# Modulation blocks moved beside the merge gates, fins held back by a count of banks, and a fixed joining time behind generators' products, in a two-layer diffusion backbone on one core

## The chip, the cores and the metric

The kernel runs on one core of a Trainium2 chip. The metric is the device time in microseconds (us). TensorE (PE in the profile) does the matrix products, VectorE (DVE) and ScalarE (ACT) the elementwise work and the reading of PSUM, GpSimd (POOL) a little of both, and SyncE's queue (SP) issues the loads.

## The reference, cut to what matters

512 tokens (256 of context, 256 latent) of width 2048 pass two layers. A layer's norm is modulated by shift and scale, and its output by a gate; all three come from a product of a 2048-vector (one for context, one for latent) with `ada_w`:

```python
shift_l, scale_l, gate_l = jnp.split((jax.nn.silu(c) @ ada_w[l] + ada_b[l])[:, None, :], 3, axis=-1)
xn_l = rmsnorm(h_lat, norm_g[l]) * (1.0 + scale_l) + shift_l
out_l, _, v_l = stream_mixer(xn_l, xn_l @ w_in[l], p, vf_lat, grid_shift, s_ctx, True)
h_lat = h_lat + gate_l * out_l
```

`stream_mixer` runs a recurrence over the tokens in both directions for 16 heads (branch A), a pooling mixer (branch B), multiplies each branch by an output matrix (`w_out_a`, `w_out_b`), weighs them with sigmoid merge gates (32 column blocks of `w_in`), adds them, and multiplies with `w_out`. In the second layer the context part ends in the state, so its outputs have 256 columns and not 512.

## The kernel before

The program is written out by a planner in Python, which keeps a clock for each engine (`E["pe"]` and so on), counts the cost of every instruction that it writes, and decides from that which comes next. What it writes is the order on each engine; on the chip the engines wait by semaphores alone.

**Main.** The large products are units in a queue (`M.q2`, and `M.q1` for those that the recurrence calls for). A unit `proj` is one block of 128 output rows; it has chunks of four 128x128 weight blocks, and each step is three matmuls (fp32 split in a high and a low fp32r part: high by high, high by low, low by high). The raw weights come by SP through a ring of three slots `wr` (512 KB each). Units write to two PSUM banks (`pmm`) in turn.

**Generators.** The recurrence is written as generators: `chain` (the walk over 8 blocks of 64 tokens for each of 8 head pairs; three product groups a block), `inv` (an inverse by doubling; some 16 product groups for each half of a pair), `prep`, `gnorm`, `open_y`. A generator yields the time at which its next step is due. Before a product that is the operand's planned time and a margin on top, `MG`, 1000 ns in layer 0 and 600 ns in layer 1. `run` (line 535 on) takes a generator whose time has come; if there is none it writes two steps of Main (six matmuls) and looks again.

**Modulation blocks.** `ada_w` is cut into 24 blocks of 256 columns for each layer: blocks 0 to 15 hold shift and scale, blocks 16 to 23 the gate. `ada_block` multiplies one as raw fp32, 4 chunks of 512 KB, each chunk four small matmuls that run beside each other in four column groups of the array. At its end (`post`) four copies bring the four partial rows to one tile `ada_r` (two on ACT, two on DVE), and a `fin` later sums them with two matmuls by `comb` and writes `modv`. With n = 2 a pair of blocks shares one bank, one set of copies and one fin. The blocks stand so:

- layer 0, blocks 0 to 15: pairs, beside the first projections (`grp`)
- layer 0, blocks 16 to 21: singly, each zipped with one merge gate product (`fillers`, only gates with i = 1); blocks 22 and 23: a pair by itself ahead of the `w_b` products (`tail`)
- layer 1, blocks 0 to 15: pairs, zipped with the 16 `w_o` products of layer 0 (`phase_b`), in banks of `piv`
- layer 1, blocks 16 and 17: a pair between the layers; 18 to 21 singly in `fillers`; 22 and 23 a pair in `tail`

`zipped` interleaves the chunks of two units, takes both units' banks before the first chunk and runs both posts after the last. `Main.step` forces all but one fin out before a unit's `pre`.

**Tail.** `open_y` starts when Main stands at a unit marked as tail; it loads the eight halves of `y_b` through four slots, splits them (`parts`), and sets `open` when all eight are written; the `w_b` units wait for `open`.

Of the kernel before, what the change touches and what calls it, by code (L numbers as in the profile page):

```python
# [18 lines left out]
T = 512  # L19
# [8 lines left out]
SC = 1024.0  # L28
WR, WH, LA, SA = 3, 3, 6, 3
NS, SL = 2, 1000  # L30
NU = (0, 1)
ZD = (0, 0)
N1, LA0, G0, LAG = 2, 20, 2, 4
AH, PACE, MG = 400.0, 600.0, (1000.0, 600.0)

V_MU, V_W0, V_A0, V_KK, V_KA, V_RK = 0, 24, 40, 56, 64, 80
# [10 lines left out]
def kernel(  # L47
# [105 lines left out]
    xn_p, py = Slots(xn_p), Slots(py)  # L153
    wr_p, wh_p, wl_p = Slots(wr_p, WR), Slots(wh_p, WH), Slots(wl_p, WH)
    pmm, piv, pch = Slots(pmm, 2), Slots(piv, 3), Slots(pch, 2)

    def psum(ap):
        return nm(ap).startswith("ps_")
# [7 lines left out]
    def mm(out, lhsT, rhs, start=True, stop=True, dep=True):  # L166
        nc.tensor.matmul(out=out, lhsT=lhsT, rhs=rhs, start=start, stop=stop)  # L167
        n, m = size(rhs), size(lhsT)
        dt = lhsT.dtype
        if dt == F32:  # L170
            c = 110 if m <= 32 else 360 if n < 32 else 1.6 * n if n > 64 else 190 if m > 64 else 78
        elif dt == R32:
            c = max(0.4225 * n, 109) + 75 * (kind[0] != dt)
        else:
            c = 28 if m > 64 else 18
        kind[0] = dt
        clk("pe", c, out, (lhsT, rhs) if dep else (), 200.0)

    kind = [R32]

    def act(out, in_, func=AF.Copy, scale=1.0, bias=None):
        kw = {} if bias is None else dict(bias=bias)
# [44 lines left out]
            late.remove(fins[0])  # L227
            fins[0][1]()

    def later(t, fn):  # L230

        x = (t, fn)
        late.append(x)
        return x

# [109 lines left out]
                    c.update(grp=dict(src=c["src"]), sl=None)  # L345
            self.ready, self.hold, self.tail = ready, hold, False

    def zipped(a, b):

        na, nb = len(a.chunks), len(b.chunks)  # L350
        order = sorted([((i + 0.5) / na, 0, i) for i in range(na)] + [((i + 0.5) / nb, 1, i) for i in range(nb)])
        pos = {(w, i): j for j, (_, w, i) in enumerate(order)}
        steps = [(pos[w, i], f) for w, u in ((0, a), (1, b)) for i, f in u.steps]

        def pre():
            for u in (a, b):
                if u.pre:
                    u.pre()

        def post():  # L360
            for u in (a, b):
                if u.post:
                    u.post()
        return Unit([(a, b)[w].chunks[i] for _, w, i in order], steps, pre, post, a.need, False, a.ready, a.hold)

    class Main:

# [81 lines left out]
        def time(self):  # L449

            self.ahead()
            if self.mi >= len(self.seq):
                return None
            c = self.seq[self.mi]
            u = c["u"]
            if c["first"] and c["pos"] == 0 and u.ready and not u.ready():
                return None
            if c["last"] and c["pos"] == len(c["steps"]) and u.need and not u.need():
                return None
            return rdy(c["r"]) if c["raw"] else rdy(c["h"], c["l"])  # L460

        def step(self):
            c = self.seq[self.mi]
            u = c["u"]
            if c["first"] and c["pos"] == 0 and u.pre:
                flush_fins(1)
                u.pre()
            if c["pos"] < len(c["steps"]):
                c["steps"][c["pos"]][1](c)
                c["pos"] += 1  # L470
            if c["pos"] == len(c["steps"]):
                if c["last"] and u.need and not u.need():
# [17 lines left out]
    def proj(src, nk, rhs, ts_, post, ck=4, **kw):  # L490
        st = {}
        n = ts_.stop - ts_.start

        def pre():
            st["ps"] = pmm.tile([128, T], F32, tag="mm", name="ps_mm")
# [19 lines left out]

    def run():

        while True:
            do_late()
            best, bt, held = None, None, True  # L520
            for g in gens:
                while g[1] is None:
                    g[1] = next(g[0], "end")
                    if g[1] is None:
                        break
                    held = False
                if g[1] == "end" or g[1] is None:
                    continue
                t = due(g[1])
                if best is None or t < bt:  # L530
                    best, bt = g, t
                if t <= E["pe"]:
                    best, bt = g, t
                    break
            gens[:] = [g for g in gens if g[1] != "end"]
            if best is None or bt > E["pe"]:
                mt = M.time()
                if mt is not None and (best is None or max(mt, E["pe"]) <= bt):
                    for _ in range(NS):
                        M.step()  # L540
                        do_late()
                        mt = M.time()
                        if mt is None or mt > E["pe"] + SL:
                            break
                    continue
            if best is None:
                if not gens and M.empty():
# [3 lines left out]
                elif held:  # L551
                    raise RuntimeError("stuck")
                continue
            E["pe"] = max(E["pe"], bt)
            best[1] = next(best[0], "end")
        do_late(True)


    def ada_blocks(l, b0, n, after=None, pre0=None, bank=None, slot=None):


        st = {}
        return [ada_block(l, b0, i, n, st, after, pre0 if i == 0 else None, bank, slot) for i in range(n)]

    def ada_block(l, b0, i, n, st, after, pre0, bank, slot):
        b = b0 + i
        nr = 2 * n

        def pre():
            if pre0:  # L570
                pre0()
            if i == 0:
                pl, tg = bank or (pmm, "mm")
                st["ps"] = pl.tile([128, T], F32, tag=tg, name="ps_ada")

        def mk(j):
            def step(c):
# [5 lines left out]
        def post():  # L583
# [3 lines left out]
            for g in range(4):  # L587
# [2 lines left out]
                    cp(ada_r[q], st["ps"][q, 0:256])  # L590
                else:
                    act(ada_r[q], st["ps"][q, 0:256])
            fins.append(later(rdy(ada_r), fin))

        def fin():

# [26 lines left out]


    def norm_sum(acc, ncol, ones):
        nc.gpsimd.memset(ones, 1.0)
        ps = piv.tile([128, T], F32, tag="iv", name="ps_nrm")
        mm(ps[:, 0:ncol], ones, acc)
        return ps[:, 0:ncol]
# [19 lines left out]
    def phase_a(l):  # L649
# [118 lines left out]
        def mix_unit(g, h):  # L768
# [1 line left out]
            st = {}  # L770

            def pre():
                st["ps"] = pmm.tile([128, T], F32, tag="mm", name="ps_mix")

            def step(c):
                for q in range(2):
# [498 lines left out]
        def open_y():  # L1275
# [7 lines left out]
            for i in range(len(todo) + 3):  # L1283
# [10 lines left out]
                if i == NP + 2:  # L1294
                    keep["open"] = True

        def load_g(f):
            if f < KD:
# [74 lines left out]
        def fillers(ada):  # L1373
# [15 lines left out]
        def tail(ada):  # L1389
# [111 lines left out]
    with tc.manual_schedule():  # L1501
# [185 lines left out]
```

## Time and profile before

| | us |
|---|---|
| three runs | 3054.97, 3052.19, 3052.75 (median 3052.75) |
| profiled execution | 3058.09 |
| its span, first to last instruction | 3056.3 |
| TensorE busy in the span | 2906.3 (95%) |
| VectorE busy | 1820.7 (60%) |
| ScalarE busy | 1457.3 (48%) |
| mean granted TensorE clock | 0.978 |

Times in rows are from the span's start. A matmul's busy time overlaps that of the next, so the step from one start to the next start is what it costs. A wait is put down to what came last. The stages by that clock: start with layer 0's modulation and first projections to about 153, recurrence and its fillers to 1380, a gap to 1401, `w_b` and `w_a` to 1599, `w_o` to 1824, the passage to layer 1 to 1860, its recurrence and fillers to 2829, a gap to 2850, and its last products to the end.

### The profile page before, as it was taken

What the parts mean: (1) busy time and instruction counts of PE and PEld (TensorE: products, weight loads), DVE (VectorE), ACT (ScalarE), POOL (GpSimd) and SP (SyncE); (2) the same over time, 40 slices, a digit from 0 to 9 for tenths busy, and PEclk for the clock granted to TensorE, in tenths of its full rate; (3) what the DMA queues carried; (4) which work ended last, traced back from release to release, by engine and by line L of the source; (5) the groups of instructions that cost most, each with busy time, mean ns of one, the idle gap of its engine ahead of it and who ended that gap; (6) DMA issues with size and microseconds to landing.
All of it is one profiled execution on the core that took longest, in us unless ns stands there. A gap on an engine that the chain in (4) does not pass through costs nothing.

```text
span 3056.3 us, 66262 instructions
## 1 busy us (share of the span) xinstructions
PE 2906.3 (95%) x27122; PEld 2292.5 (75%) x27122; DVE 1820.7 (60%) x4171; ACT 1457.3 (48%) x3092; POOL 149.7 (5%) x211
## 2 busy tenths in 40 slices
PE   5999999999999999998999989999999989999897
PEld 2687777767777777776876657887887768888797
DVE  3475666565655655534443235886786667775575
ACT  3254445445554554533222223666556646666454
POOL 2200000000000000000000002000000000000000
PEclk8999999999999999998999999999999989999899
DMA  9732222232333222327657764432333343344875
GB/s 361 256 121 72 78 76 91 72 116 94 112 111 118 87 80 87 94 88 248 205 190 225 234 222 124 141 117 85 108 94 111 119 127 99 111 122 129 260 251 161
DMA packets 158482, 427.74 MB, mean 140 GB/s; under 512 B 17376, under 2 KB 53600, under 8 KB 154080
## 3 DMA queue, kind: packets, MB, share of 16 engines
q1 hardware_dynamic: 133120, 390.32, 40.5%
q10 hardware_dynamic: 25056, 33.17, 3.0%
q8 instruction: 213, 3.49, 0.5%
q14 instruction: 93, 0.76, 0.1%
HBM read 389.21 MB, written 34.21 MB: 139 GB/s over the span
## 4 chain that ended last, share of the span: by engine, by line
PE 78%; DVE 8%; DMA 7%; ACT 5%; issue 2%; SPq 0%; POOL 0%; DVEq 0%; ACTq 0%; POOLq 0%
PE ps_mm L167 54%; PE ps_st L167 4%; DMA wr<-in_w_o 3%; DVE wlo L191 3%; PE ps_W L167 3%; PE ps_M L167 2%; PE ps_ada L167 2%; PE ps_y L167 2%; PE ps_a L167 2%; DMA wr<-in_w_in 2%; PE ps_Z L167 1%; PE ps_z L167 1%; PE ps_p L167 1%; ACT whi L183 1%; PE ps_T L1113 1%
## 5 line engine op out<-in xcount | busy, mean ns | idle before, releaser
L167 PE MATMUL ps_mm<-xh,whi 128*128 128x512 f32 (+1 forms) x2448 | 914.8, 374 | 8.2 <-ACT whi L183 3.1
L191 DVE TENSOR_TENSOR wlo<-wr,whi 128x512 fp32r<-128x512 f32 (+1 forms) x932 | 636.7, 696 | 444.8 <-ACT whi L183 439.1
L183 ACT ACTIVATE whi<-wr 128x512 fp32r<-128x512 f32 (+1 forms) x932 | 567.1, 619 | 671.3 <-PE ps_mm L167 336.7
L167 PE MATMUL ps_mm<-xh,wlo 128*128 128x512 f32 (+1 forms) x2448 | 855.2, 349 | 16.4 <-DVE wlo L191 15.7
L167 PE MATMUL ps_mm<-xl,whi 128*128 128x512 f32 (+1 forms) x2448 | 851.1, 348 | 0.0
L167 PEld LDWEIGHTS ps_mm<-xh,whi 128*128 128x128 f32 x2448 | 465.6, 190 | 91.9 <-issue 7.9
L167 PEld LDWEIGHTS ps_mm<-xh,wlo 128*128 128x128 f32 x2448 | 465.8, 190 | 83.5 <-DVE wlo L191 22.5
L167 PEld LDWEIGHTS ps_mm<-xl,whi 128*128 128x128 f32 x2448 | 467.6, 191 | 46.3 <-issue 1.0
L167 PE MATMUL ps_mm<-mgh,whi 128*128 128x512 f32 (+1 forms) x512 | 181.2, 354 | 2.9 <-ACT whi L183 2.9
L1024 DVE CAST_PREDICATED X<-pm_t,ps_W 128x128 f16<-128x128 uint8 x640 | 141.7, 288 | 65.2 <-PE ps_W L167 63.8
L167 PE MATMUL ps_mm<-mgh,wlo 128*128 128x512 f32 (+1 forms) x512 | 175.4, 343 | 0.0
L167 PE MATMUL ps_mm<-mgl,whi 128*128 128x512 f32 (+1 forms) x512 | 174.5, 341 | 0.0
L167 PE MATMUL ps_mm<-yh,whi 128*128 128x512 f32 (+1 forms) x512 | 129.0, 344 | 0.2 <-ACT whi L183 0.2
L167 PEld LDWEIGHTS ps_mm<-mgh,whi 128*128 128x128 f32 x512 | 98.2, 192 | 38.9 <-issue 19.3
L167 PE MATMUL ps_mm<-yl,whi 128*128 128x512 f32 (+1 forms) x512 | 125.4, 337 | 0.6 <-DVE m L195 0.5
L183 ACT ACTIVATE VS<-P 64x128 f32<-64x128 f32 x128 | 39.3, 307 | 167.3 <-DVE P L195 164.8
L183 ACT ACTIVATE zb<-ps_Z 128x512 f16<-128x512 f32 x144 | 85.2, 592 | 70.2 <-PE ps_Z L167 68.8
L167 PEld LDWEIGHTS <-X 64*64 64x64 f16 x2560 | 89.4, 110 | 35.7 <-issue 27.5
L191 POOL TENSOR_TENSOR nlo<-MM,n 64x512 f16<-64x512 f32 x48 | 62.8, 1308 | 1072.2 <-DVE X L1024 760.2
L167 PEld LDWEIGHTS ps_mm<-mgh,wlo 128*128 128x128 f32 x512 | 98.3, 192 | 14.5 <-DVE wlo L191 3.6
L167 PEld LDWEIGHTS ps_mm<-mgl,whi 128*128 128x128 f32 x512 | 98.4, 192 | 8.7
L167 PE MATMUL ps_ada<-wr,svp 128*4 128x256 f32 (+1 forms) x1024 | 83.2, 402 | 22.8 <-DMA wr<-in_ada_w 22.8
(258 smaller groups left out, 4353.2 us busy)
## 6 DMA issues: line engine op xcount, KB each, us to landing
wr<-in_w_in SPq DMA_DIRECT2D x306, 512.0 KB, 3.7
wr<-in_ada_w SPq DMA_DIRECT2D x128, 512.0 KB, 3.9
wbig<-in_ada_w SPq DMA_DIRECT2D x32, 1024.0 KB, 6.0
wr<-in_w_o SPq DMA_DIRECT2D x64, 512.0 KB, 4.8
wr<-in_w_b SPq DMA_DIRECT2D x32, 512.0 KB, 4.8
wr<-in_w_a SPq DMA_DIRECT2D x32, 512.0 KB, 4.0
wr<-in_w_st SPq DMA_DIRECT2D x32, 384.0 KB, 4.3
d_mg<-mth ACTq DMA_DIRECT2D x32, 256.0 KB, 2.0
```

The costliest lines, as they stand in the source:

```text
L167: nc.tensor.matmul(out=out, lhsT=lhsT, rhs=rhs, start=start, stop=stop)
L183: nc.scalar.activation(out=out, in_=in_, func=func, scale=scale, **kw)
L191: ENG[eng].tensor_tensor(out=out, in0=a, in1=b, op=op)
L1024: nc.vector.copy_predicated(dst.rearrange(pat, **kw)[:, :, :, u, :], m, src.rearrange(pat, **kw)[:, :, :, u, :])
L1113: nc.tensor.transpose(ps[:, j2, d, :], BK[:, d, c % 4].rearrange("p a t -> p (a t)"), ident)
```

## The change

- In `run`, while products of a generator (or a fin) stand behind the last batch of Main, a generator that is due within `JOIN` = 600 ns of the planner's TensorE clock is taken at once and not after the next two steps of Main. The planner's TensorE clock no longer jumps to the due time for a step with products.
- All gate blocks of layer 0 and blocks 0 to 15 of layer 1 (24) go singly, zipped with merge gates of layer 0: both gates of f = 0 to 7 and the gate i = 1 of f = 8 to 15. Layer 1's blocks 18 to 23 (6) go singly in its fillers. The `tail` pairs and the blocks beside `w_o` are gone. These zips have `lead` 0.25: the modulation chunk stands ahead of the gate's chunk.
- `zipped` calls each unit's `pre` at its own first step and its `post` at its own last step.
- `bank` counts the banks of `pmm` taken, and forces out a fin only when its bank is the one to be taken next. A fin without `after` is due `FD` = 400 ns later than before.
- A `w_b` chunk waits for its own four halves of `y_b` and no more for all eight.
- The memset of `ones` in `norm_sum` (three times in all) moves from GpSimd to VectorE.

```diff
+FD = 400.0
+JOIN = 600.0
+    def bank(name):
+        while fins and fins[0][2] <= taken[0] - 2:
+            flush_fins(len(fins) - 1)
+        taken[0] += 1
+        return pmm.tile([128, T], F32, tag="mm", name=name)
...
-    def zipped(a, b):
+    def zipped(a, b, lead=0.5):
-        order = sorted([((i + 0.5) / na, 0, i) for i in range(na)] + [((i + 0.5) / nb, 1, i) for i in range(nb)])
+        order = sorted([((i + 0.5) / na, 0, i) for i in range(na)] + [((i + lead) / nb, 1, i) for i in range(nb)])
+            def first(c, f=ls[0][1], u=u):
                 if u.pre:
                     u.pre()
+                f(c)
+            def final(c, f=ls[-1][1], u=u):
+                f(c)
                 if u.post:
                     u.post()
...
+            if "ready" in c and not c["ready"]():
+                return None
             if c["first"] and c["pos"] == 0 and u.pre:
-                flush_fins(1)
                 u.pre()
...
+        was = -1
         while True:
             do_late()
+            now = E["pe"] + (JOIN if count[0] != was else 0)
...
-                if t <= E["pe"]:
+                if t <= now:
                     best, bt = g, t
                     break
-            if best is None or bt > E["pe"]:
+            if best is None or bt > now:
...
+                    was = count[0]
                     continue
...
-            E["pe"] = max(E["pe"], bt)
+            n = count[0]
+            if bt > now:
+                E["pe"] = bt
             best[1] = next(best[0], "end")
+            if count[0] == n:
+                E["pe"] = max(E["pe"], bt)
...
-            fins.append(later(rdy(ada_r), fin))
+            fins.append(later(rdy(ada_r) + (0 if after else FD), fin, st["n"]))
...
-        nc.gpsimd.memset(ones, 1.0)
+        nc.vector.memset(ones, 1.0)
...
-                    q.append(zipped(u, ada.pop(0)) if i and ada else u)
+                    q.append(zipped(u, ada.pop(0), 0.25) if (i or len(ada) > KD - 1 - f) and ada else u)
...
-            for u in ada:
-                u.hold, u.tail = free, True
-            q = list(ada)
+            q = []
-                u = proj(w_b[l, f], NP, lambda k: keep["yh"][k], slice(0, nt), post_b(f), hold=free,
-                         ready=lambda: "open" in keep)
+                u = proj(w_b[l, f], NP, lambda k: keep["yh"][k], slice(0, nt), post_b(f), hold=free)
+                for i, c in enumerate(u.chunks):
+                    c["ready"] = lambda i=i: "yh" in keep and all(keep["yh"][4 * i:4 * i + 4])
...
-        M.q2 += A[0]["fillers"](sum((ada_blocks(0, KD + j, 1) for j in range(6)), []))
-        M.q2 += A[0]["tail"](ada_blocks(0, 22, 2))
-        ada1 = sum((ada_blocks(1, b, 2, bank=(piv, "iv")) for b in range(0, KD, 2)), [])
-        qb, B0 = phase_b(0, lambda: A[0], lambda f: hT[f], lambda f: ada1[f])
+        M.q2 += A[0]["fillers"](sum((ada_blocks(0, KD + j, 1) for j in range(8)), []) +
+                                sum((ada_blocks(1, j, 1) for j in range(KD)), []))
+        M.q2 += A[0]["tail"]()
+        qb, B0 = phase_b(0, lambda: A[0], lambda f: hT[f], lambda f: None)
...
-            M.q2 += a["fillers"](sum((ada_blocks(1, KD + N1 + j, 1) for j in range(4)), []))
-            M.q2 += a["tail"](ada_blocks(1, 22, 2))
+            M.q2 += a["fillers"](sum((ada_blocks(1, KD + N1 + j, 1) for j in range(6)), []))
+            M.q2 += a["tail"]()
```

## Rows read from the trace of the kernel before

**Rows 1.** Stretches: us, busy PE, PEld, DVE, ACT, POOL; PEclk, DMA share, GB/s

```profile
153.00:1380.00 1227.00, 1218.37 (x11316) 921.83 (x11315) 720.66 (x1676) 595.70 (x1264) 43.99 (x55) 1.00 0.30 95
1380.00:1401.00 21.00, 7.63 (x72) 2.14 (x70) 8.65 (x14) 7.78 (x14) 0.00 (x0) 0.68 0.80 263
...
1599.00:1824.00 225.00, 214.43 (x1188) 138.71 (x1188) 67.44 (x137) 47.11 (x86) 0.00 (x0) 0.98 0.70 227
...
1860.00:2829.00 969.00, 931.55 (x11091) 796.73 (x11089) 704.87 (x1761) 586.08 (x1317) 62.00 (x78) 0.98 0.38 114
2829.00:2850.00 21.00, 8.67 (x76) 2.96 (x75) 6.79 (x16) 7.36 (x19) 0.00 (x0) 0.64 0.75 242
...
1401.00:1404.60 3.60, 3.60 (x10) 2.92 (x10) 3.40 (x8) 2.09 (x4) 0.00 (x0) 0.50 0.07 16
...
2850.00:2855.20 5.20, 5.20 (x25) 5.20 (x26) 3.75 (x11) 2.16 (x6) 0.00 (x0) 0.50 0.46 129
```

**Rows 2.** TensorE's waits (us, times, longest) in 153:1380, 1599:1824 and, two rows, 1860:2829

```profile
PE ps_ada L167 <- DVE ada_r L206: 4.5, 6, 2.1
...
PE ps_ada L167 <- DVE ada_r L206: 8.7, 7, 1.5
...
PE ps_mm L167 <- DVE wlo L191: 14.4, 15, 2.2
...
PE ps_ada L167 <- DVE ada_r L206: 2.8, 2, 1.8
```

**Rows 3.** Timeline of TensorE: first matmuls of six-matmul stretches, and one group

```profile
256.21 0.50 PE L167 MATMUL ps_mm<-xh,whi 128*128 128x512 f32 x1
...
1299.19 0.50 PE L167 MATMUL ps_mm<-xh,whi 128*128 128x512 f32 x1
...
1979.06 0.28 PE L167 MATMUL ps_mm<-xh,whi 128*128 128x256 f32 x1
...
2789.22 0.28 PE L167 MATMUL ps_mm<-xh,wlo 128*128 128x256 f32 x1
2789.43 0.45 PE L167 MATMUL ps_z<-VS,MM 128*64 128x64 f32 x8
2789.82 0.39 PE L167 MATMUL ps_mm<-xh,whi 128*128 128x256 f32 x1
2790.04 0.28 PE L167 MATMUL ps_mm<-xl,whi 128*128 128x256 f32 x1
2790.16 0.28 PE L167 MATMUL ps_mm<-xh,wlo 128*128 128x256 f32 x1
```

**Rows 4.** Timeline of TensorE around one modulation chunk beside `w_o`

```profile
1819.58 0.39 PE L167 MATMUL ps_mm<-mgh,wlo 128*128 128x512 f32 x1
1819.90 0.61 PE L167 MATMUL ps_ada<-wr,svp 128*4 128x256 f32 x8
1820.44 0.50 PE L167 MATMUL ps_mm<-mgh,whi 128*128 128x512 f32 x1
```

**Rows 5.** Timeline: first and last of one post's four copies, and its fin

```profile
1825.13 0.37 ACT L183 ACTIVATE ada_r<-ps_ada 4x256 f32<-4x256 f32 x1
...
1826.71 0.43 DVE L206 COPY ada_r<-ps_ada 4x256 f32<-4x256 f32 x1 [0.44 <-ACT ada_r L183]
...
1827.54 0.61 PE L167 MATMUL ps_ada<-comb,ada_r 128*128 128x4 f32 x4
```

**Rows 6.** Loads of `y_b` on SP's queue; the page's group of low parts

```profile
1374.36 1.85 SPq L263 DMA_DIRECT2D ldp<-d_yb  x4
...
L191 DVE TENSOR_TENSOR wlo<-wr,whi 128x512 fp32r<-128x512 f32 (+1 forms) x932 | 636.7, 696 | 444.8 <-ACT whi L183 439.1
```

**Rows 7.** The start: TensorE's first products, and two stretches

```profile
22.40 2.07 PE L167 MATMUL ps_nrm<-acc,ones 128*128 128x512 f32 x2 [22.40 <-POOL ones L626]
...
22.00:26.00 4.00, 3.60 (x22) 1.10 (x26) 0.69 (x1) 0.73 (x2) 0.34 (x2) 1.00 1.01 428
26.00:30.00 4.00, 2.80 (x52) 0.91 (x40) 2.58 (x4) 1.62 (x3) 0.00 (x0) 1.00 0.98 346
```

More of the change, by code (lines that the diff above doesn't have):

```diff
@@ L155 @@
     pmm, piv, pch = Slots(pmm, 2), Slots(piv, 3), Slots(pch, 2)
+    taken = [0]
+    def bank(name):
[3 more added lines that the diff above has]
+        return pmm.tile([128, T], F32, tag="mm", name=name)
     def psum(ap):
@@ L176, in mm @@
         kind[0] = dt
+        count[0] += 1
         clk("pe", c, out, (lhsT, rhs) if dep else (), 200.0)
-    kind = [R32]
+    kind, count = [R32], [0]
     def act(out, in_, func=AF.Copy, scale=1.0, bias=None):
@@ L228, in flush_fins, with later @@
             fins[0][1]()
-    def later(t, fn):
-        x = (t, fn)
+    def later(t, fn, n=0):
+        x = (t, fn, n)
         late.append(x)
@@ L346, in __init__ @@
             self.ready, self.hold, self.tail = ready, hold, False
-    def zipped(a, b):
+    def zipped(a, b, lead=0.5):
         na, nb = len(a.chunks), len(b.chunks)
-        order = sorted([((i + 0.5) / na, 0, i) for i in range(na)] + [((i + 0.5) / nb, 1, i) for i in range(nb)])
+        order = sorted([((i + 0.5) / na, 0, i) for i in range(na)] + [((i + lead) / nb, 1, i) for i in range(nb)])
         pos = {(w, i): j for j, (_, w, i) in enumerate(order)}
-        steps = [(pos[w, i], f) for w, u in ((0, a), (1, b)) for i, f in u.steps]
-        def pre():
-            for u in (a, b):
+        steps = []
+        for w, u in ((0, a), (1, b)):
+            ls = [(pos[w, i], f) for i, f in u.steps]
+            def first(c, f=ls[0][1], u=u):
                 if u.pre:
                     u.pre()
-        def post():
-            for u in (a, b):
+                f(c)
+            def final(c, f=ls[-1][1], u=u):
+                f(c)
                 if u.post:
                     u.post()
-        return Unit([(a, b)[w].chunks[i] for _, w, i in order], steps, pre, post, a.need, False, a.ready, a.hold)
+            ls[0] = (ls[0][0], first)
+            ls[-1] = (ls[-1][0], final)
+            steps += ls
+        return Unit([(a, b)[w].chunks[i] for _, w, i in order], steps, None, None, a.need, False, a.ready, a.hold)
     class Main:
@@ L494, in pre @@
         def pre():
-            st["ps"] = pmm.tile([128, T], F32, tag="mm", name="ps_mm")
+            st["ps"] = bank("ps_mm")
         def mk(k):
@@ L553, in run, with ada_blocks, ada_block @@
                 continue
-            E["pe"] = max(E["pe"], bt)
+            n = count[0]
+            if bt > now:
+                E["pe"] = bt
             best[1] = next(best[0], "end")
+            if count[0] == n:
+                E["pe"] = max(E["pe"], bt)
         do_late(True)
-    def ada_blocks(l, b0, n, after=None, pre0=None, bank=None, slot=None):
+    def ada_blocks(l, b0, n, after=None, pre0=None, slot=None):
         st = {}
-        return [ada_block(l, b0, i, n, st, after, pre0 if i == 0 else None, bank, slot) for i in range(n)]
-    def ada_block(l, b0, i, n, st, after, pre0, bank, slot):
+        return [ada_block(l, b0, i, n, st, after, pre0 if i == 0 else None, slot) for i in range(n)]
+    def ada_block(l, b0, i, n, st, after, pre0, slot):
         b = b0 + i
@@ L572, in pre @@
             if i == 0:
-                pl, tg = bank or (pmm, "mm")
-                st["ps"] = pl.tile([128, T], F32, tag=tg, name="ps_ada")
+                st["ps"], st["n"] = bank("ps_ada"), taken[0] - 1
         def mk(j):
@@ L772, in pre @@
             def pre():
-                st["ps"] = pmm.tile([128, T], F32, tag="mm", name="ps_mix")
+                st["ps"] = bank("ps_mix")
             def step(c):
@@ L1293, in open_y @@
                     parts(todo[i - 3][0], todo[i - 3][2], ys[i - 3])
-                if i == NP + 2:
-                    keep["open"] = True
         def load_g(f):
@@ L1385, in fillers, with tail @@
                     u = proj(win(50 + 16 * i + f), KD, rhs, yts, post_mg(i, f))
-                    q.append(zipped(u, ada.pop(0)) if i and ada else u)
+                    q.append(zipped(u, ada.pop(0), 0.25) if (i or len(ada) > KD - 1 - f) and ada else u)
             return q
-        def tail(ada):
+        def tail():
             free = lambda: not M.q1
-            for u in ada:
-                u.hold, u.tail = free, True
-            q = list(ada)
+            q = []
             for f in range(KD):
-                u = proj(w_b[l, f], NP, lambda k: keep["yh"][k], slice(0, nt), post_b(f), hold=free,
-                         ready=lambda: "open" in keep)
+                u = proj(w_b[l, f], NP, lambda k: keep["yh"][k], slice(0, nt), post_b(f), hold=free)
                 u.tail = True
+                for i, c in enumerate(u.chunks):
+                    c["ready"] = lambda i=i: "yh" in keep and all(keep["yh"][4 * i:4 * i + 4])
                 if f == 0:
```

## The prediction, made before the changed kernel was run

> **What bounds the kernel now.** I read the stretches first, to find where TensorE is not the limit, then its waits in each stretch, then the timeline where the change works. In layer 0's recurrence (153 to 1380) TensorE is busy 1218 of 1227 us at full clock, with VectorE at 59% and ScalarE at 49% [rows 1]. So the order of products there costs nothing in waits; what it can still cost is the change from one kind of product to another. In layer 1's recurrence (1860 to 2829) TensorE is busy 932 of 969 us, and VectorE 73%: some 37 us are idle, of which the largest group is low parts of weights (`wlo`) that come late, 14.4 us in 15 waits [rows 1, 2]. Two gaps of 21 us, behind the two recurrences, have TensorE busy 7.6 and 8.7 us, at a mean granted clock of 0.68 and 0.64, with the DMA engines at 0.80 and 0.75 [rows 1]: there the pair of modulation blocks in `tail` runs as fast as its 4 MB come. Beside `w_o` (1599 to 1824) it is fins that TensorE waits for, 8.7 us in 7 waits [rows 2].
>
> **Joined products.** The price of a change of kind is in one group. From the last Main matmul (2789.22) to the group takes 0.21 us where 256 columns step by 0.12 (2790.04 to 2790.16): 0.09 more. The first Main matmul behind it takes 0.22 to the next: 0.10 more [rows 3]. A group that is drawn into the one ahead of it saves 0.19 us. What can be drawn in is what now waits for one batch of Main and then comes at once. Counted in the timeline, 100 stretches of Main between two groups are six matmuls long in layer 0 (the first begins at 256.21, the last at 1299.19) and 145 in layer 1 (1979.06 to 2789.82) [rows 3]. All other stretches are longer: the next step there was due more than a batch later. A 512-column step is 0.23 (0.32 from 1819.58 to 1819.90, less the 0.09 of entering [rows 3, 4]), so a six is 6 x 0.23 + 0.1, about 1.5 us in layer 0. In layer 1, 72 of the 145 are of 256 columns, 0.9 us, and 73 of 512. If the due times lie evenly in these stretches, 600 ns takes 0.4 of 100, 0.67 of 72 and 0.41 of 73: 40 + 48 + 30 = 118 groups, 118 x 0.19 = 22.4 us. Bounds: none of them, 0; all 245, 46.6 us.
>
> Against it stands what a joined product waits for. In layer 0 a product is due 1000 ns behind its operand's planned time, so 600 ns less leaves 400. In layer 1 the margin is 600, and nothing is left: there 78 joined groups may wait whenever the plan is early by anything. Of layer 1's 37.4 us idle, 14.4 are low parts and 2.8 fins [rows 1, 2]; the 20 left are other operands and evacuations. There are 304 groups there, and 78 of them, a quarter, would be joined: I add a quarter of the 20, 5 us. Below it is 0; above see the second rival. The change also moves the elementwise steps of generators ahead by up to 600 ns on VectorE and ScalarE, where Main's splits stand behind them; in layer 0, with 41% of VectorE free, I take nothing for it. **Joined: 22.4 - 5.0 = 17.4 saved.**
>
> **Sixteen blocks from `w_o` to the merge gates.** A chunk costs, from the Main matmul ahead of it to the one behind, 0.86 us, less that matmul's own 0.23, and 0.10 on the way out: 0.73 us [rows 4]. The 64 chunks cost this in the one place as in the other, since both are bound by TensorE and interleaved four to a product; their loads (2 MB a block) brought no DMA wait beside `w_o` at 227 GB/s [rows 1, 2], and the recurrence moves 95. What differs are the fins. The stage at `w_o` loses 8 fins of 0.6 + 0.19 = 0.8 us [rows 3, 5], 6.4 together, their 8.7 us of waits, and the pauses that took the granted clock to 0.98, 2% of 225 us, 4.5: 19.6 us. Single blocks need 16 fins in their place. Why fins wait is seen at one post: the four copies run one behind the other over two engines, from 1825.13 to 1827.14, 2.0 us, the last one having waited for ScalarE [rows 5], where the planner counts two on each engine side by side. In the recurrence the six fins of layer 0 waited 4.5 us, 0.75 each [rows 2]; `FD` sends them 0.4 later, which leaves 0.35. So 16 x (0.8 + 0.35) = 18.4, and **1.2 saved**. For the ten fins that already stand in the recurrences, 4.5 + 2.8 us of waits [rows 2] become 3.5: **3.8 saved**. If the copies run no faster beside the gates than at `w_o` (8.7 / 7 = 1.25 us late), 0.85 is left at each of 30 fins; if `FD` covers all, nothing: 15 us more or 10 less.
>
> Taking each bank at its unit's own first chunk puts four small matmuls between a gate's last product and the bank's next use, in place of none; but all of TensorE's idle time in layer 0's recurrence is 8.6 us, 4.5 of it fins [rows 1, 2], so no more than 4.1 can be banks: I take 0.
>
> **The two tails.** Each gap ends with 21.0 us gone, and the products behind it begin at the lower of the clock's two levels, 1.2 of 2.4 GHz: 3.6 us in layer 0 and 5.2 in layer 1 at 0.50 [rows 1], half of it lost: 1.8 and 2.6. Two blocks move into the recurrence: 8 x 0.73 and 2 x 1.15, 8.2 us. What is late next is `y_b`: with no pair to run, TensorE stands still until the first four halves are split. The last gate's evacuation (one ScalarE operation, some 0.6), one high part and four low parts of 0.70 [rows 6] are 4.0; the loads were issued at 1374.4, 6 us ahead of the gap [rows 6], and so do not count; the last pair's `gnorm` shares both engines: 6 us. Below, 3; above, 12, if the planner's 3.5 us for a load and its `gnorm` steps come ahead of the splits. The clock will still fall in 6 us of rest: 2 more. Layer 0: 21.0 + 1.8 - 8.2 - 8 = 6.6; layer 1: 21.0 + 2.6 - 8.2 - 8 = 7.4. **14.0 saved** (bounds 3 and 20). If the second pair's cover were still needed, it would be for the chain, but the chain's products were at their end in both gaps.
>
> **The memset.** TensorE's first product waits to 22.40 for `ones`, behind GpSimd's other work [rows 7]. It looks large and is not: the stage runs on the loads of `ada_w`, at 428 GB/s from 22 to 26. Only the dip to 346 behind it, 4 x 82 / 428 = 0.8 us, can be won [rows 7]. The other two memsets now follow the last sum on VectorE, 0.1 each: **0.6 saved** (0 to 0.8).
>
> **The sum.** 17.4 + 1.2 + 3.8 + 14.0 + 0.6 = 37.0 us. The profiled execution took 3058.1, which is 5.3 above the median of the runs, 3052.75. 3058.1 - 37.0 = 3021.1, less 5.3 is **3016 us** for the runs.
>
> **Rivals.**
> *Joining wins nothing.* The due times lie behind 600 ns, or a stall eats each saved change. For it: most stretches, 176 of layer 0's 337, are twelve long, so steps tend to be due two batches later. Against: 100 are not. 3016 + 17.4 = 3033.
>
> *The elementwise queues are blocked, and it ends slower.* A generator's step that is taken 600 ns early puts operations on VectorE whose inputs are not there, and the splits for the next chunks stand behind them. Layer 1 has VectorE at 73% and already waits for `wlo` 15 times [rows 1, 2]. At 0.25 us for each of its 304 groups it is 76 us: 3033 + 76, about 3109. It decides from 3033 to 3053: 20 us, 0.07 us for each group in layer 1. The Trainium skill, "TensorE: Matmul & The Clock Gate", in the paragraph on engine queue depths, says that ScalarE and VectorE are strict FIFO and that TensorE alone reorders, and only its weight loads. By that rule an early step delays everything behind it by its full earliness, and the whole of a mean 0.3 us at 304 groups, 91 us, would be open to TensorE; that `wlo` is what layer 1 waits for agrees, that it does so at 15 of 304 groups speaks for a buffer of splits ahead that takes up most of it.
>
> *Fins stay late.* 0.85 us at each of 30 fins in place of 0.35: 3031.
>
> *The ring of three slots.* Twenty-four zipped products in a row want six 512 KB loads each through three slots. A wait of 0.5 us at each chunk would be 32 us: 3048. Against it: `w_o` ran so, without such a wait.
>
> *All goes better.* 245 joins without stalls and pauses of 3 us: 3016 - 29 - 6 - 10, about 2970; half of it, 2993.
>
> **Chances.** The forecast, 2996 to 3030: 0.52. Joining wins nothing, 3030 to 3040: 0.14. Fins stay late or tails stay long, 3025 to 3045: 0.07. The ring: 0.05, half of it under 3046. Blocked queues: 0.10, with 0.01 of it near no change. Better, under 2996: 0.12, a third of that under 2985. 0.2% is 6 us, about what a measurement of this kernel can tell from no change: 3046.6 to 3058.9 is "same". Faster: 0.52 + 0.14 + 0.07 + 0.12 + 0.01 = 0.86; same 0.05; slower 0.09. From 2985 to 3045 leaves out 0.04 below and some 0.14 above.
>
> **What would show it.** Fewer changes of kind: about 300 groups in layer 0's recurrence where 337 are, 225 in layer 1 where 304 are, and stretches of six turned scarce. `w_o` in some 178 us with TensorE never waiting. The gaps at the tails 5 to 7 us and not 21. TensorE's wait for `ones` near 19 us, and the first merge products no more than 1 us earlier. Wrong I would be by waits of the `ps_z`, `ps_a`, `ps_W` products in layer 1 well over 20 us together, by waits for `wlo` over 25, by `ps_ada` waiting for DMA inside layer 0's recurrence, or by `y_b` splits queued behind `gnorm` for 10 us and more.

## The result and the profile after

| | before | after |
|---|---|---|
| runs, median (lowest to highest), us | 3053.86 (3052.19 to 3055.18) | 3085.84 (3079.41 to 3089.95) |
| profiled execution and its span, us | 3058.09, 3056.3 | 3089.05, 3087.3 |
| TensorE busy, us | 2906.3 (95%) | 2920.9 (95%) |
| mean granted TensorE clock | 0.978 | 0.976 |

The changed kernel is 1.0100 times as long, interval 1.0084 to 1.0116: 32 us slower, where 37 us faster was forecast. The table below gives the length of each stage from its first product to the next stage's first, worked out from the TensorE rows of the two traces; in brackets what TensorE stood idle and how long the clock was at its lower level.

| stage, us | before | after | change |
|---|---|---|---|
| start | 152.2 | 150.0 | -2.2 |
| recurrence, layer 0 | 1227.7 (8.6; 3.4) | 1318.8 (35.6; 13.7) | +91.1 |
| gap, then `w_b` | 21.2 + 88.8 | 2.1 + 93.6 | -14.3 |
| `w_o` | 248.9 (11.6; 10.2) | 176.8 (0; 0) | -72.1 |
| recurrence, layer 1 | 919.4 (37.5; 37.5) | 962.9 (58.8; 75.1) | +43.5 |
| gap, then `w_b` | 20.9 + 49.7 | 3.0 + 53.5 | -14.1 |

All other stages together are 0.9 us shorter. The same stretches of after, as [rows 1] showed them of before (length; busy us of PE, PEld, DVE, ACT, POOL; granted clock, DMA share, GB/s):

```profile
150.00:1469.00 1319.00, 1283.44 (x11969) 940.28 (x11967) 748.37 (x1774) 610.88 (x1307) 43.59 (x55) 0.99 0.38 117
1469.00:1471.00 2.00, 0.28 (x2) 0.12 (x1) 0.14 (x1) 1.80 (x4) 0.00 (x0) 1.00 0.17 69
...
1651.80:1828.60 176.80, 174.24 (x769) 144.01 (x769) 66.52 (x111) 46.33 (x76) 0.00 (x0) 1.00 0.41 127
1910.70:2873.70 963.00, 904.25 (x10930) 775.31 (x10928) 682.54 (x1732) 573.69 (x1294) 46.83 (x55) 0.96 0.38 113
...
1471.00:1476.00 5.00, 4.54 (x12) 3.03 (x12) 2.96 (x5) 1.39 (x3) 0.00 (x0) 0.68 0.65 180
...
2876.60:2886.00 9.40, 6.99 (x28) 5.50 (x29) 4.58 (x11) 3.93 (x10) 0.00 (x0) 0.63 0.56 182
```

`w_o` is what it should be: full clock, and TensorE waits for nothing between its first and its last product (the 2.6 us that are not busy in its row are the wait for the norm behind the last one). Of the gaps 2.1 and 3.0 us are left. Both recurrences took up more than was saved. In layer 1's recurrence the mean granted clock is 0.96 where before had 0.98 [rows 1]. TensorE's waits of after (us in all, times, longest), first the longest of layer 0's recurrence, then of layer 1's; [rows 2] are those of before:

```profile
PE ps_ada L177 <- DVE ada_r L217: 15.4, 14, 3.4
PE ps_mm L177 <- DVE v L206: 3.5, 3, 1.2
...
PE ps_T L1137 <- DVE X L1048: 11.8, 4, 4.2
PE ps_mm L177 <- DVE wlo L202: 9.8, 12, 2.2
PE ps_ada L177 <- DVE ada_r L217: 7.2, 5, 1.5
PE ps_z L177 <- ACT VS L194: 3.8, 3, 1.8
PE ps_M L177 <- DVE MM L202: 3.8, 10, 0.8
PE ps_a L177 <- ACT Zs L194: 2.8, 4, 1.8
```

In the recurrences the fins wait three times as long as before (22.6 us where 7.3 were), low parts of weights less than before, and many operands of generators' products are new in the list. I sort all such rows of a recurrence into four kinds: fins (`ada_r`), generators' products, weights, and banks (a large product or a modulation product that waits for an evacuation). Of generators' products before had 1.2 us in 2 waits in layer 0 and 12.5 in 16 in layer 1; after has 11.8 in 16 and 35.6 in 48.

One more thing that the waits do: in layer 1's recurrence of after the granted clock fell to half 15 times, each time with a wait of TensorE of 1.1 to 4.2 us just over or still running. Not each such wait brought a fall: there were 22 of 1.1 us or more. Half clock for 75.1 us in place of before's 37.5 is 18.8 us lost, beside the 21.3 us by which idle time grew.

### The profile page after: what moved, and what is told of

It reads as the page before. It is cut to its first block, busy times and chain, and to the rows that moved or that the text cites. A ratio compares the mean times of both kernels' runs of the same rounds, so it can differ in the third digit from the quotient of the medians.

```text
span 3087.3 us, 66404 instructions
## 1 busy us (share of the span) xinstructions
PE 2920.9 (95%) x27162; PEld 2316.3 (75%) x27162; DVE 1832.6 (59%) x4222; ACT 1464.1 (47%) x3112; POOL 149.8 (5%) x208
## 5 line engine op out<-in xcount | busy, mean ns | idle before, releaser
L177 PE MATMUL ps_mm<-xh,whi 128*128 128x512 f32 (+1 forms) x2448 | 918.2, 375 | 10.6 <-DVE v L206 3.5
L177 PEld LDWEIGHTS ps_mm<-xh,wlo 128*128 128x128 f32 x2448 | 471.1, 192 | 79.4 <-DVE wlo L202 17.8
L177 PE MATMUL ps_mm<-mgh,whi 128*128 128x512 f32 (+1 forms) x512 | 172.0, 336 | 0.0
L177 PEld LDWEIGHTS ps_mm<-yh,whi 128*128 128x128 f32 x512 | 92.3, 198 | 23.3 <-ACT yh L194 9.1
```

## The experiments

Times are medians; before stood at 3053.1 to 3055.5 in every set of runs. Lengths of stages and waits are of the one profiled execution of each kernel, which lies up to 5 us off its median.

**Joining, taken out and put in alone.** Taken out: `JOIN = 0.0` in the changed kernel. Put in alone: the new `run` in the kernel before, with nothing else of the change.

> The changed kernel with JOIN at 0 and all else as changed. Theory A (joined products wait for operands that are not there) and theory B (elementwise steps taken early, which push the planner's clock and fill the queues, spoil the order) both put the loss into the joining: without it the other parts of my sum remain, 19.6 us saved, less 12 because fins waited 0.75 us each and not 0.35, so about 3046 us. Theory C (the blocks in the recurrence cost more than they did beside w_o, and the joining helps): about 3100, the 17 us of the joining lost again.

> The kernel before with only the new rule in run (JOIN 600). A and B: slower, by about 40 us, 3094. C: faster by 17, 3037.

Without joining 3060.15 (1.0023, 1.0013 to 1.0032); joining alone 3078.7 (1.0085, 1.0065 to 1.0105). So joining costs 25.7 us in the one kernel and 25.6 in the other (3078.7 less 3053.09), and the rest of the change loses 7.1 (3060.15 less 3053.09) where 19.6 were to be won. Most of the loss is the joining's, as theories A and B had it, but both kernels missed the times that I had expected, 3046 and 3094. Joining alone leaves layer 0's recurrence nearly as long (1232.0) and lengthens layer 1's from 919.4 to 942.3.

Without joining, too, layer 1's recurrence (940.9) is 21.5 us longer than before's, with two more modulation blocks in it; 13.8 of this is idle time. Waits for banks grew from 4.0 to 12.2 us and those of generators' products from 12.5 to 19.4. Three of the rows of the kernel without joining, in layer 1's recurrence:

```profile
PE ps_T L1137 <- DVE X L1048: 9.3, 4, 3.8
...
PE ps_mm L177 <- DVE modv L202: 4.8, 4, 1.9
PE ps_mm L177 <- DVE r L206: 4.4, 3, 1.7
```

**Joining, by its parts.** Three versions of the changed kernel. The first takes a step ahead of its time only when it has products (a step whose due time holds the margin, or that comes as a pair with a count); an elementwise step is taken when it is due (the main lines of the edit):

```diff
-                if t <= now:
-                    best, bt = g, t
+                if t <= (now if isinstance(g[1], (tuple, Due)) else E["pe"]):
+                    best, bt, got = g, t, True
```

The second joins every kind of step, but an elementwise one no longer moves the planner's TensorE clock to its due time (two polls are spaced 700 instead of 500 ns):

```diff
             best[1] = next(best[0], "end")
-            if count[0] == n:
-                E["pe"] = max(E["pe"], bt)
```

The third keeps all of joining and sets `MG` to (1600, 1200).

> The changed kernel with joining for steps with products alone; elementwise steps come at their own due time as before and push the clock only as before. A: no better than the changed kernel, 3080 to 3090, since it is the products that wait. B: the saved changes of kind remain and the loss goes, 3025 to 3040.

> The changed kernel, with elementwise steps still joined but no longer pushing the planner's TensorE clock to their due time (two polls of 500 ns become 700, so that they end). Theory B1 (the pushed clock, 118 us of planned idle time that the chip doesn't spend, misplaces what follows): falls to about e3_products, 3056. Theory B2 (the early place in the queues of VectorE and ScalarE does it): stays at 3075 or more.

> The changed kernel as it is, joining of every kind of step and its push of the planner's clock kept, with the margin between an operand's planned time and its product raised from 1000 and 600 ns to 1600 and 1200. Theory A (joined products go out ahead of operands that are still under way on the chip, because joined elementwise steps push the planner's clock ahead of the chip, and layer 1's 600 ns margin is all eaten by the 600 ns of joining): layer 1's recurrence, 963 us, falls by 20 us or more, TensorE's idle time there from 59 to about 40; in all 3060 to 3068. Theory B (what costs is that a push lets VectorE and ScalarE work be written in a worse order, which no margin mends): 3080 or more.

| | us | recurrence 0 (waits of generators' products) | recurrence 1 (idle; half clock; these waits) |
|---|---|---|---|
| after | 3085.84 | 1318.8 (11.8) | 962.9 (58.8; 75.1; 35.6 in 48) |
| products alone joined | 3055.71 | 1326.9 (4.1) | 922.6 (40.0; 37.5; 17.8 in 27) |
| clock not moved | 3049.54 | 1319.3 (4.2) | 927.3 (48.9; 17.1; 18.0 in 33) |
| larger margin | 3064.98 | 1306.0 (2.5) | 906.3 (49.0; 47.8; 16.9 in 25) |
| no joining | 3060.15 | 1309.3 (2.8) | 940.9 (51.3; 37.5; 19.4 in 16) |

The first version lies between what theory A (3080 to 3090) and theory B (3025 to 3040) had expected; it is 4.4 us faster than no joining. The second version decides between the two ways in which elementwise steps could cost. It takes them ahead of their time by the same rule as after, and it is 36.3 us faster. So what costs is not in the main that early operations block VectorE and ScalarE, but the planner's clock. When an elementwise step was joined, the planner set its TensorE clock forward to the step's due time, with no product written in between. Counted in the planner as it wrote the program, this happened 240 times in layer 0 and 216 in layer 1 and added 66.8 and 51.4 us of rest that the chip doesn't take. By that much products were thought to be later than they are, and they came ahead of their operands. (Without the moved clock fewer steps fall within the 600 ns: 153 and 162 are still taken early, by 0.26 us on average as before.)

By the profiles nearly all of the gain lies in layer 1's recurrence, where the margin is 600 ns. In layer 0 the recurrence stays as long (1319.3 for 1318.8): its generators' products wait 4.2 us in place of 11.8, but its waits for banks grow from 3.5 to over 16. What joining costs in layer 0 without the one copy shown below, 9.5 us in after (1318.8 less 1309.3), is thus not put down to the moved clock by this run. The row of the second version's recurrence in layer 1, at a mean granted clock of 0.99 where after had 0.96:

```profile
1911.20:2838.40 927.20, 878.25 (x10928) 750.02 (x10928) 683.78 (x1732) 573.91 (x1294) 45.97 (x55) 0.99 0.38 117
```

Of the 35.6 us by which this stretch is shorter, the clock accounts for some 29 (58.0 us less at its lower level, half of it lost) and idle time for 9.9; some 3 us of after's idle time fell into half clock and count twice here. The larger margin gives back 20.9 of the 36, within what theory A had expected (3060 to 3068), and cuts the waits of generators' products as far; but here some 22 product groups come too late for the gates and stand beside `w_b` (81.9 us for 53.5, with a gap of 14.5). What the joining of elementwise steps costs beyond the lost margin is not told apart by it.

Not all of the 35.6 us that generators' products wait in layer 1 of after is due to joining: 11.8 are `ps_T`, which waits for a bank of the inverse that `X` still reads, and it does so for 9.3 without joining too.

**What a merged group is worth.** To the `w_a` products of layer 0 of the kernel before, small groups are added, in the one kernel 128 by themselves and in the other the same products as 64 merged ones:

```diff
+                if k % 2 == 0:
+                    group(F32)
+                if k % 2:
+                    group(F16)
```

The merged kernel has `k % 2` in both conditions. These products (four of fp32 or eight of fp16, 64x64) go to a bank that nothing reads.

> The price of a change of kind by itself, with no waits: the kernel before with small products added in layer 0's w_a stage, where no generator runs. Behind every even step four 64x64 fp32 products, behind every odd step eight 64x64 fp16 products, into a bank that nobody reads: 128 groups. About 0.95 us a pair of groups, 64 of them, 61 us: 3114.

> The same added products, but the fp32 group and the fp16 group stand together behind every odd step: 64 groups. If a merged group saves 0.19 us, as I took it, 12 us less than x1_apart. If the change between fp32 and fp16 costs the same inside a group as the way over Main does, the two agree within 4 us.

3124.81 (1.0225; I had expected 3114) and 3104.2 (1.0159). The `w_a` stretch of the kernel with groups by themselves:

```profile
1491.00:1644.90 153.90, 153.90 (x1409) 94.72 (x1407) 52.88 (x80) 28.40 (x48) 0.20 (x1) 1.00 0.33 109
```

and of the merged one:

```profile
1493.40:1627.60 134.20, 134.20 (x1409) 96.53 (x1407) 53.05 (x80) 28.36 (x48) 0.20 (x1) 1.00 0.37 125
```

The same 1409 products, never idle, at full clock: 19.7 us for 64 merges, 0.31 us each; in medians 20.6, where I had expected 12. A merged group is worth more than the 0.19 that I took, when nothing waits.

**Fins.** Five kernels. `FD` = 1600 without joining; and, in four bases, one copy for four: the modulation product is made with 32 columns of `svp` for each column group, so that all 128 rows of the bank are written, and one ScalarE operation brings them to `ada_r`:

```diff
-            for g in range(4):
-                q = slice(32 * g, 32 * g + nr)
-                if g % 2:
-                    cp(ada_r[q], st["ps"][q, 0:256])
-                else:
-                    act(ada_r[q], st["ps"][q, 0:256])
+            act(ada_r, st["ps"][:, 0:256])
```

> The changed kernel with JOIN at 0 and FD at 1600 ns and not 400. If fins wait because the four copies take 2.0 us where the planner counts a third of that, their 22.6 us of waits fall to under 5 and the time to about 17 below e1_nojoin, near 3029. Rival: copies wait behind other work in their queues and not for each other, so a fixed 1.2 us more leaves half of the waits, 3038 or more.

> e3_products with one ScalarE copy of all 128 rows of ps_ada in place of four copies of 2 to 4 rows on two engines (the weights' slice is 32 columns wide, so all rows are written; comb has zeros for the rest). If fins wait because the four copies run one behind the other (2.0 us), their waits, 16 us, nearly vanish and the time is about 3042. Rival: they wait behind other work in the queues, then 3052.

> The kernel before with only the one copy in place of four. By the copies' own time the 25.9 us that TensorE waits for ada_r fall to some 5, and the clock stays up in w_o: about 3030. If they wait for other work, 3048.

> e4_nopush with the one copy of e8_onecopy. If the two repairs are of different losses they add up: 3050 - 40 = about 3010, the fastest so far. If the pushed clock mattered because fins came at wrong times, the gain overlaps: 3015 to 3025.

> e1_nojoin with the one copy: no joining at all. If joining, once repaired, is worth the 17 us of my sum, this is 17 above e12_nopush_copy, about 3027. If merging groups saves next to nothing, the two are within 6 us.

| one copy in | without it, us | with it, us | difference | ratio to the kernel before (interval) |
|---|---|---|---|---|
| the kernel before | 3054.11 | 3031.89 | -22.2 | 0.9924 (0.9904 to 0.9945) |
| no joining | 3060.15 | 3030.86 | -29.3 | 0.9924 (0.9908 to 0.9941) |
| clock not moved | 3049.54 | 3022.80 | -26.7 | 0.9899 (0.9878 to 0.9920) |
| products alone joined | 3055.71 | 3015.18 | -40.5 | 0.9869 (0.9848 to 0.9890) |

`FD` = 1600 gave 3052.41 (0.9995, 0.9985 to 1.0005), 7.7 under no joining: fins in layer 0 waited 1.0 us in place of 10.3, but waits for banks grew from 8.7 to 19.3, since a later fin holds its bank longer; so neither 3029 nor 3038 and more, which I had expected, came about. The timeline of one post of after, with its fin:

```profile
726.91 0.38 ACT L194 ACTIVATE ada_r<-ps_ada 2x256 f32<-2x256 f32 x1 [3.65 <-PE ps_ada L177]
727.32 0.42 DVE L217 COPY ada_r<-ps_ada 2x256 f32<-2x256 f32 x1 [1.24 <-ACT ada_r L194]
727.77 0.38 ACT L194 ACTIVATE ada_r<-ps_ada 2x256 f32<-2x256 f32 x1 [0.48 <-DVE ada_r L217]
728.18 0.43 DVE L217 COPY ada_r<-ps_ada 2x256 f32<-2x256 f32 x1 [0.44 <-ACT ada_r L194]
728.66 0.52 PEld L177 LDWEIGHTS ps_ada<-comb,ada_r 128*128 128x128 f32 x4 [0.66 <-DVE ada_r L217]
728.66 0.61 PE L177 MATMUL ps_ada<-comb,ada_r 128*128 128x2 f32 x4 [0.23 <-DVE ada_r L217]
```

From the second on, each copy waits for the one on the other engine (the bracket), 1.7 us from first start to last end, and nothing else runs on its engine meanwhile. The same post with one copy (and products alone joined):

```profile
721.58 0.39 ACT L194 ACTIVATE ada_r<-ps_ada 128x256 f32<-128x256 f32 x1 [3.38 <-PE ps_ada L177]
722.71 0.64 PEld L177 LDWEIGHTS ps_ada<-comb,ada_r 128*128 128x128 f32 x4
722.93 0.50 PE L177 MATMUL ps_ada<-comb,ada_r 128*128 128x2 f32 x4
```

128 rows take as long as two, and in this kernel TensorE waits for no fin in either recurrence. The gain, 40.5 us, is larger than the 16.0 us of waits for fins that it takes away: the start, whose pairs use the same copies, is 4.7 us shorter, and in layer 1 the time at half clock falls from 37.5 to 13.7 us. I had expected 3042 and have no full account of the 27 us beyond it. The two repairs don't add up, either: with one copy the kernel whose clock is not moved, which still takes elementwise steps early, is 7.6 us slower than the one that joins products alone, where without the copy it is 6.2 faster. Why is open.

**The move from `w_o`.** Without joining, layer 1's blocks 0 to 15 go back beside `w_o` in pairs, but in `pmm` banks and not in `piv`:

```diff
-        qb, B0 = phase_b(0, lambda: A[0], lambda f: hT[f], lambda f: None)
+        ada1 = sum((ada_blocks(1, b, 2) for b in range(0, KD, 2)), [])
+        qb, B0 = phase_b(0, lambda: A[0], lambda f: hT[f], lambda f: ada1[f])
```

> The changed kernel with JOIN at 0 and layer 1's blocks 0 to 15 back in pairs beside w_o (now in pmm banks); the tails stay changed. If the move is neutral, as my sum had it (1.2 us saved, the fins' longer waits taking it back), 3058 to 3062, like e1_nojoin. If the blocks cost more in the recurrence, by banks held and evacuations waited for, 3045 to 3052.

3102.92 (1.0153, 1.0128 to 1.0179). Layer 0's recurrence is 1239.0 in place of 1309.3, so the 16 blocks cost 70.3 us there. As a price of the place beside `w_o` this run fails (I had expected 3045 to 3062), because its banks are not those of before; its waits from 1560 to 1900 say why `w_o` took 280.2 us:

```profile
PE ps_ada L177 <- DVE ada_r L217: 28.8, 7, 5.3
...
PE ps_mm L177 <- DVE hn L206: 5.9, 8, 1.9
```

**Layer 0, and the lead.** Two versions of the fastest kernel so far (one copy, products alone joined, 3015.18): joining in layer 1 alone, and the zips' `lead` back at 0.5.

```diff
-            now = E["pe"] + (JOIN if count[0] != was else 0)
+            now = E["pe"] + (JOIN if A[1] and count[0] != was else 0)
```

```diff
-                    q.append(zipped(u, ada.pop(0), 0.25) if (i or len(ada) > KD - 1 - f) and ada else u)
+                    q.append(zipped(u, ada.pop(0), 0.5) if (i or len(ada) > KD - 1 - f) and ada else u)
```

> The one-copy kernel with joining of product steps in layer 1 alone; layer 0 takes its steps when they are due, as the kernel before does. It tells what joining is worth in layer 0, where 40 fewer groups stand beside more bank waits. Theory A (fewer groups there pay 0.32 us each less the waits, so something is won): layer 0's recurrence, 1304 us with joining, grows to 1308 to 1316, 3019 to 3027 in all. Theory B (in layer 0 the waits for banks and the clock eat what the fewer groups save): layer 0's recurrence stays at 1300 to 1306, 3011 to 3018 in all.

> The one-copy kernel that joins product steps alone, with the 24 and 6 zips at lead 0.5 again, so that a gate's first chunk stands ahead of the modulation chunk. At lead 0.25 a gate that follows a projection takes that projection's bank behind four small matmuls; twice in layer 0 TensorE waited 4.5 us for it, because the evacuation stood on ScalarE and VectorE behind a generator's operations. Theory A (lead 0.25 is what takes a bank early): those two waits of 9.0 us go, layer 0's waits for banks fall from 16.4 to 5 to 9, and the time from 3015 to 3004 to 3009. Theory B (any zip takes a bank early, since the gate behind a zip follows its last modulation chunk in either order): waits for banks stay at 13 or more and the time within 3011 to 3020.

Joining in layer 1 alone: 3020.51 (0.9881, 0.9862 to 0.9899), layer 0's recurrence 1308.3 with 339 groups where joining there has 1304.0 with 297. So 42 fewer groups win 4.3 us, 0.10 each. Both runs came out as theory A had it. Lead 0.5: **3003.46** (0.9830, 0.9814 to 0.9847), 11.7 us under lead 0.25 and the fastest kernel of this study. What lead 0.25 did is seen in the timeline of the kernel that has it:

```profile
954.44 0.40 PE L177 MATMUL ps_mm<-xh,wlo 128*128 128x512 f32 x1
...
954.77 0.64 PE L177 MATMUL ps_ada<-wr,svp 128*32 128x256 f32 x8
...
956.12 0.31 ACT L194 ACTIVATE VS<-P 64x128 f32<-64x128 f32 x1 [5.01 <-DVE P L206]
...
958.25 0.67 ACT L194 ACTIVATE v<-ps_mm,vx_t 128x512 f32<-128x512 f32 x1
...
958.95 0.81 DVE L206 SCALAR_TENSOR_TENSOR v<-ps_mm,ve_t,v 128x255 f32<-128x255 f32 x2 [2.61 <-ACT v L194]
...
959.90 0.77 PE L177 MATMUL ps_mm<-xh,whi 128*128 128x512 f32 x1 [4.50 <-DVE v L206]
```

A projection has ended in one of the two banks (its last product, 954.44, is over at 954.84); the modulation block takes the other, and behind its eight small products the gate wants the first. But the projection's evacuation (`v`) stands on ScalarE behind `VS`, which had ScalarE wait until 956.12 for `P`, and behind three more operations; it begins at 958.25, 3.4 us after its data lay ready. With lead 0.5 the gate takes the free bank, and the block takes the projection's one gate chunk, twelve large products, later. In layer 0's recurrence the waits for banks fall from 16.4 to 8.4 us, all of them the gates' own evacuations now (the two waits for `v` of the kernel with lead 0.25, then all waits for banks of the one with lead 0.5):

```profile
PE ps_mm L177 <- DVE v L206: 9.0, 2, 4.5
...
PE ps_mm L177 <- ACT mth L194: 8.4, 9, 2.1
```

The Trainium skill, "TensorE: Matmul & The Clock Gate", paragraph on engine queue depths, calls ScalarE and VectorE strict FIFO; these rows agree: an evacuation whose data lay ready at 954.84 stood behind an operation that waited until 956.12 for its own operand.

## Why the prediction was wrong

**Joined products** ("17.4 saved"). The count was right: I forecast 118 groups drawn in; 339 + 306 groups without joining are 292 + 238 with it, 115 fewer. The price of a group, 0.19, was not too large where nothing waits (0.31). The step that failed is the sentence on elementwise steps: "in layer 0, with 41% of VectorE free, I take nothing for it", with no term for them in layer 1 either, where the margin is 600 and the joining time is 600. I looked at them as load on VectorE; what they do is to move the planner's clock, two lines that stand in the diff, 456 times and by 118 us. With the clock left alone the same kernel is 36.3 us faster, by the profiles nearly all of it in layer 1, so there the missing term counted most. The 5 us of waits that I did take were the joined products' own. Measured: 25.7 us lost, not 17.4 saved. Joining of products alone saves 4.4 in the changed kernel (3060.15 to 3055.71) and 15.7 with one copy (3030.86 to 3015.18, at 115 fewer groups, 339 + 315 to 297 + 242, 0.14 each; 3.3 in layer 0's recurrence and 13.6 in layer 1's by their profiles). Joining of all steps with the clock left alone saves 10.6 and, with one copy, 8.1. So the 17.4 came near only for products alone and once the fins were mended; in the changed kernel other waits took most of it.

**Fins** ("1.2 saved", "3.8 saved"). `FD` was to leave 0.35 us at each of 30 fins, 10.5 in all. After has 22.6 in 19 waits, 0.75 for each of the 30, as much as layer 0's six fins waited in the kernel before; the rival "Fins stay late" had 0.85. My reading of [rows 5], copies one behind the other, was right, and I stopped there: I took the delay of the fin for the remedy, where the copies themselves were it. They cost 22 us in the kernel before as well, where TensorE waited for fins 4.5, 8.7 and 2.8 us in the three stretches of [rows 2].

**Banks** ("I take 0", "no more than 4.1"). In the changed kernel itself 3.5 us of layer 0's waits are for banks, within the bound, but 8.7 without joining. The bound was wrong in kind: idle time of the kernel before bounds what banks cost there, not in an order in which a gate follows a projection by four or eight small products. In the kernels with one copy and lead 0.25 layer 0's recurrence waits 16 to 19 us for banks, where the kernel before with one copy waits 0.6. That eats what moves and tails bring: with one copy and no joining the change is worth 1.0 us (3031.89 to 3030.86), where I had 19.6; the move has less to bring there, too, since `w_o` of the kernel before with one copy takes 236.8 and not 248.9. The edit to `lead` I priced not at all; it was 11.7 us of it.

**The move** was neutral, as said: `w_o` gives 72.1 us, sixteen blocks cost 70.3. **The tails** ("14.0 saved") held for the pause: with the lower clock it cost 2.1 + 4.8 us in layer 0 and 3.0 + 3.8 in layer 1 beside the `w_b` of before, which had lost 1.8 and 2.6 to the clock itself; so 8.7 and 9.4 in all for the 8 that I took. What failed is the price of two blocks, 8.2. In layer 0's recurrence they cost 11.3 (1239.0 against 1227.7), and the tail brings 3.0 where 6.6 was forecast. In layer 1's they came with 21.5 more (no joining, 940.9 against 919.4), so that this tail loses 8.3 by the profiles where it was to save 7.4; with one copy it is 6.2 (924.5 against 918.3), and the tail saves 7.5. By the profiles most of what the rest of the change missed of its 19.6 lies in this second tail, in waits of layer 1's recurrence for which I had no term. **The memset** brought the first product from 22.40 to 18.75. The stage is 2.2 us shorter in after, but 0.5 to 1.4 in the other kernels with the memset and four copies, so the 0.6 that I took is not refuted; no run has the memset alone. The row of after's timeline that answers to [rows 7]:

```profile
18.75 2.08 PE L177 MATMUL ps_nrm<-acc,ones 128*128 128x512 f32 x2 [18.75 <-DVE ones L650]
```

**The rivals.** The one that ends slower, blocked queues, was nearest in time and wrong in mechanism: none of its signs came (`ps_z`, `ps_a` and `ps_W` wait 14.4 us together, under its 20; `wlo` 9.8, under its 25). Early elementwise steps without the moved clock cost nothing that is seen with four copies (3049.54 against 3055.71 with products alone), but 7.6 us with one copy (3022.80 against 3015.18); whether that is blocked queues no run tells. The ring of three slots brought no DMA wait in layer 0.

In medians, from after to the fastest: 3085.84, products alone joined -30.1, one copy -40.5, lead 0.5 -11.7, 3003.46. Open stays why one copy wins more than its fins' waits in layer 1, where only six blocks stand, what the moved clock costs beyond the lost margin, and what joining costs layer 0 with four copies.

## What to carry to other kernels

When a planner takes work ahead of its due time, look at what each kind of taken step does to the planner's own clock: here steps that write nothing on TensorE advanced its clock, and each of them ate of the margin of the products that follow. A wait that is short in the profile can stand for an arrangement that costs several times as much; before delaying the waiter, shorten what it waits for. And the idle time of the old order is no bound for a resource (here two banks) that the new order takes sooner.

## What the runs showed of the hardware

One ScalarE copy of 128 rows takes 0.39 us, one of 2 rows 0.38; four copies of 2 rows to one tile from two engines take 1.7 us, the last three with 1.24, 0.48 and 0.44 us of waiting for the other engine in their brackets. Eight small products with 32 columns on their stationary side took 0.64 us, with four columns 0.61 [rows 4]. And a late operand could cost more than its wait: a wait of 1.1 to 4.2 us stood at each of the 15 falls of the clock to half in layer 1 of the changed kernel, though 7 of the 22 waits of that length brought none.
